# Hybrid decoder layer on one core: the gate projection as one product per k tile, the modulation sums in two halves

## The chip, the cores and the metric

One core of a Trainium2 chip runs the whole layer in one launch. The metric is the device time in microseconds (us) of that launch; three runs were made of the kernel before. Beside them stands one profiled execution with a trace of every instruction.

## What is computed

The layer takes x (256 tokens by 2048), a conditioning vector c and the weights, all float32. Cut to what matters here:

```python
mod = silu(c) @ w_mod + b_mod                  # six sections of 2048
sh_m, sc_m, g_m, sh_f, sc_f, g_f = split(mod, 6)
h = rmsnorm(x, mix_pre_w) * (1 + sc_m) + sh_m
proj = h @ w_in                                # 2048 x 6160
cb, cc, cx, q, k, v, r, a_lr = split(proj)     # a_lr: the last 16 columns
log_a = log_sigmoid(a_lr @ gate_w2 + gate_b) / 16
y = concat(conv(cb, cc, cx), gated_linear_attention(q, k, v, log_a, r)) @ w_out
x = x + g_m * rmsnorm(y, mix_post_w)
x = x + g_f * rmsnorm(conv_ffn(rmsnorm(x) * (1 + sc_f) + sh_f), ffn_post_w)
```

The change touches the 16 columns a_lr (the gate projection) and the place of the sums that turn w_mod's partial products into sh_m and sc_m.

## The kernel before

**Numbers.** Products of large matrices are made from float32 operands split into a high part (rounded to the reduced format float32r by a copy on ScalarE, ACT) and a low part (operand minus high part, a subtraction on VectorE, DVE). A product is then three matmuls on TensorE (PE): high times high, high times low, low times high (L476 to L478 in the input projection). Weights: `high` (L140, ACT, tile `wh`) and `low` (L145, DVE, tile `wl`). Activations: `act_high` (L362, ACT) and `act_low` (L366, DVE) fill the tile `hts[k // 2]`, which holds for each k tile the 256 high columns and, right behind, the 256 low ones.

**Units.** The work is a list of units; `drive` (L69) writes out all instructions in program order, and each engine takes its own in that order. A unit loads a block of weights on SyncE's (SP's) queue two units ahead (`prep`, with the ACT copy), splits it one unit ahead (`low`, DVE), and multiplies (`mm`, PE). Around these stand lists to which other work is hung: `early` (before the next units' prep and low), `pre` (before mm), `mid` (behind mm), then `fin` of the unit before (its results leave PSUM: L402 on DVE), then `late`. So DVE's stream runs one unit ahead of PE's in `low`, and what stands in `late` of unit i stands on DVE behind `low` of unit i + 1.

**Input projection.** The 16 k tiles (128 rows each) are taken in four chunks of 2, 4, 5 and 5 (`CHUNKS`). This text numbers the units: chunk 0 is units 0 to 11, chunk 1 units 12 to 23 (48 matmuls each), chunk 2 units 24 to 41 (45 or 30 matmuls each; unit 24 has 45), chunk 3 units 42 to 59; then 16 units of the output projection (60 to 75), the feed-forward up projection and the down projection. All 12 groups of 512 projection columns stay in SBUF as sums that each chunk adds to.

**Modulation.** While a chunk is multiplied, DVE builds the next chunk's sh_m and sc_m: `mod_steps` multiplies each loaded block of w_mod by a column of silu(c) and adds (L136, into the tile `macc`). Two units before the chunk ends (`LEAD` = 2: units 10, 22 and 40) the 128 partitions are summed by matmuls with a matrix of ones as the moving operand, two columns wide (`products`, L284; `macc` stands as the weights). Each such float32 matmul appears in the trace as two records. `products` for both sections stand in `early` of that unit, ahead of its mm; `columns` (L287, L288, DVE) takes the sums out of PSUM in `late`, and `first` of `modulate_chunk` follows there: PE transposes the normalised x (L347), ACT scales and shifts it (L353) and makes the high part (L362).

**Gate projection.** `second` of `modulate_chunk` multiplies the float32 weights `alr_w` (16 columns) with the float32 activations, one matmul per k tile (L422, two records each), and issues `act_low` (L366) of the chunk. It stands in `late` of the chunk's last unit ahead (units 11, 23, 41); for chunk 0 it stands before the units. `third` (L430, L432, DVE) adds the 16 rows to the tile `alr` in `mid` of the chunk's first unit (12, 24, 42). After chunk 3 the gate steps `gla_gate0` to `gla_gate4` use `alr` with `gate_w2` and a row of ones for `gate_b`.

Of the kernel before, what the change touches and what calls it, by code (L numbers as in the profile page):

```python
# [6 lines left out]
F32 = mybir.dt.float32  # L7
F32R = mybir.dt.float32r
# [6 lines left out]
P = 128  # L15
# [88 lines left out]
def layer_kernel(ctx: ExitStack, tc, x, c, w_mod, b_mod, mix_pre_w, mix_post_w, w_in, conv_w, gate_w2, gate_b,  # L104
# [18 lines left out]
    def slot(shape, dt=F32):  # L123
        return big.tile(shape, dt, tag="big", name=nm("big"))
# [77 lines left out]
    NSV = 58  # L202
    sv_r = const.tile([NSV, P], F32, tag="sv_r", name="sv_r")
    sv = col(NSV, "sv")
# [21 lines left out]
    gla = {}  # L226
    alr_w = const.tile([P, KT, 16], F32, tag="alr_w", name="alr_w")

# [6 lines left out]
    def load_gate():  # L235
        gw = gla["w"] = slot([17, 512])
        nc.gpsimd.dma_start(gw[0:16, :], gate_w2[0])
        nc.gpsimd.dma_start(gw[16:17, :], gate_b)

# [145 lines left out]
    proj = {}  # L385
    alr = const.tile([17, T], F32, tag="alr", name="alr")
    nc.gpsimd.memset(alr, 1.0)
# [16 lines left out]
    def modulate_chunk(ci, ash, early=None):  # L404

        k0, k1 = bounds[ci], bounds[ci + 1]
        kept = []

        def first():
            for kts in pairs(k0, k1):  # L410
                ps = early.pop(0) if early else turn_norm(xs, kts)
                hf = hf0[:, kts[0]:kts[-1] + 1, :] if ci == 0 else hf_tile()
                modulate(ps, kts, ash, CHUNKS[ci], k0, hf)
                for i, k in enumerate(kts):
                    h32.setdefault(ci, {})[k] = hf[:, i, :]
                kept.append((kts, hf, act_high(kts, hf, hts)))

        def second():
            ps = bank([P, T])
            for kts, hf, parts in kept:  # L420
                for i, k in enumerate(kts):
                    nc.tensor.matmul(ps[:16, :], alr_w[:, k, :], hf[:, i, :], start=(k == k0), stop=(k == k1 - 1))  # L422
                if parts:
                    act_low(*parts)
            kept.append(ps)

        def third():
            ps = kept.pop()
            if ci == 0:
                nc.vector.tensor_copy(alr[:16, :], ps[:16, :])  # L430
            else:
                nc.vector.tensor_add(alr[:16, :], alr[:16, :], ps[:16, :])  # L432

        return first, second, third

# [530 lines left out]
    for j, f in enumerate(steps0):  # L966
# [5 lines left out]
        if j in NLD:  # L972
# [5 lines left out]
            nc.scalar.activation(xs[t][1], xs[t][1], AF.Copy, scale=r)  # L978
    nc.sync.dma_start(alr_w, w_in[:, 6144:6160].rearrange("(k p) n -> p k n", p=P))
    small_columns()  # L980
# [5 lines left out]
    columns()  # L986
    for f in modulate_chunk(0, ash, early):
        f()
# [10 lines left out]
    for ci in range(1, len(CHUNKS)):  # L999
# [6 lines left out]
        def cols(ci=ci, n=n, st=st):  # L1006
            st["ash"], products, st["columns"] = mod_columns(st["accs"], n, pre_c[:, bounds[ci]:bounds[ci + 1]], f"ash{ci}")
            products()

        def mod0(ci=ci, st=st):  # L1010
# [265 lines left out]
```

## Time and profile before

| what | us |
|---|---|
| median of 3 runs | 1220.81 |
| lowest, highest | 1220.12, 1221.87 |
| the profiled execution's own time | 1220.69 |
| its span in the trace | 1218.9 |
| PE busy | 1178.1 |
| DVE busy | 947.4 |
| ACT busy | 569.6 |

Times in the trace count from the span's start; 1.8 us of the profiled execution's time lie around the span. Engines: PE is TensorE's matmuls, PEld its weight loads, DVE VectorE, ACT ScalarE, POOL GpSimd, SP SyncE. A row of the timeline gives start, duration, engine, line, operation, output and inputs, shape, count, and in brackets the idle time before it with what ended it. A row of the chain gives start, length, engine and line of merged pieces. A row of the table of windows gives, for a stretch of the span, its length, the busy time and count of PE, PEld, DVE, ACT and POOL, the granted clock of TensorE as a share of full speed, the share of the DMA engines and GB/s. Matmuls are pipelined, so their durations overlap: the pace is the distance between starts.

### The profile page before, as it was taken

The numbers are of one execution on the slowest core, as the hardware profiler recorded it, in microseconds if no ns is written. First come the engines' busy times: TensorE is split into PE (matmuls) and PEld (weight loads), VectorE is DVE, ScalarE is ACT, GpSimd is POOL, SyncE is SP. The second block draws the span as 40 slices with busy tenths as digits, with TensorE's granted clock in tenths as the row PEclk, the third lists the DMA queues.
The fourth block names the chain that finished last, engine by engine and source line by source line (L and its number), as shares of the span: only waits on it lengthen the run. The fifth ranks groups of instructions, "written<-read, shape, count | busy, mean of one in ns | idle before, by whom it ended". The sixth has DMA issues, their size and how long they took to land.

```text
span 1218.9 us, 17103 instructions
## 1 busy us (share of the span) xinstructions
PE 1178.1 (97%) x6993; PEld 1043.1 (86%) x6993; DVE 947.4 (78%) x966; ACT 569.6 (47%) x665; POOL 31.9 (3%) x49
## 2 busy tenths in 40 slices
PE   2999999999999999999999999999999999999997
PEld 1999999999997888888888888888888888888885
DVE  5999899999999877885598979698876664444464
ACT  5553432453474446444564545544545543443442
POOL 2000020000001000000000000000000000000000
PEclk9999999999999998999999999999999999999999
DMA  9999899996699985996766767767674665555522
GB/s 306 385 390 389 306 361 394 397 333 210 203 338 365 341 315 199 355 344 230 240 216 240 249 228 236 261 214 269 220 232 154 241 252 184 204 185 195 199 77 69
DMA packets 128046, 320.73 MB, mean 263 GB/s; under 512 B 8341, under 2 KB 35685, under 8 KB 118240
## 3 DMA queue, kind: packets, MB, share of 16 engines
q1 hardware_dynamic: 125360, 312.63, 72.2%
q0 software_dynamic: 2320, 6.94, 1.5%
q8 instruction: 55, 0.90, 0.3%
q14 instruction: 23, 0.19, 0.0%
q10 hardware_dynamic: 288, 0.07, 0.0%
HBM read 315.42 MB, written 4.19 MB: 262 GB/s over the span
## 4 chain that ended last, share of the span: by engine, by line
PE 94%; DMA 3%; DVE 2%; issue 1%; ACT 0%; SPq 0%; DVEq 0%; ACTq 0%
PE ps L882 27%; PE ps L884 14%; PE ps L741 9%; PE ps L740 9%; PE ps L739 9%; PE ps L476 7%; PE ps L478 7%; PE ps L477 7%; DMA raw<-in_w_mod_dram 2%; PE ps L571 1%; PE ps L473 1%; DVE big L136 1%; PE ps L284 1%; PE ps L422 1%; PE ps L1135 1%
## 5 line engine op out<-in xcount | busy, mean ns | idle before, releaser
L140 ACT CAST wh<-raw 128x2048 fp32r<-128x2048 f32 (+3 forms) x202 | 366.3, 1815 | 507.1 <-PE ps L882 195.3
L145 DVE TENSOR_TENSOR wl<-raw,wh 128x2048 fp32r<-128x2048 f32 (+3 forms) x202 | 437.5, 2167 | 142.3 <-ACT wh L140 142.3
L882 PE MATMUL ps<-big,wh 128*128 128x512 f32 x1400 | 494.8, 398 | 1.8 <-DVE big L366 1.8
L884 PE MATMUL ps<-big,wl 128*128 128x256 f32 x1400 | 393.4, 281 | 0.0
L882 PEld LDWEIGHTS ps<-big,wh 128*128 128x128 f32 x1400 | 263.6, 188 | 65.7 <-DVE big L366 2.1
L884 PEld LDWEIGHTS ps<-big,wl 128*128 128x128 f32 x1400 | 265.2, 189 | 0.0
L478 PE MATMUL ps<-big,wl 128*128 128x256 f32 x733 | 210.0, 286 | 3.5 <-DVE wl L145 3.5
L476 PE MATMUL ps<-big,wh 128*128 128x256 f32 x733 | 211.5, 289 | 0.2 <-ACT wh L140 0.2
L477 PE MATMUL ps<-big,wh 128*128 128x256 f32 x733 | 209.5, 286 | 0.0
L136 DVE SCALAR_TENSOR_TENSOR macc<-raw,c_act,macc 128x2048 f32<-128x2048 f32 (+1 forms) x96 | 199.4, 2077 | 1.8 <-DMA raw<-in_w_mod_dram 1.7
L739 PE MATMUL ps<-wh,big 128*128 128x512 f32 x456 | 178.3, 391 | 0.0
L740 PE MATMUL ps<-wl,big 128*128 128x512 f32 x456 | 177.5, 389 | 0.0
L741 PE MATMUL ps<-wh,big 128*128 128x512 f32 x456 | 177.5, 389 | 0.0
L478 PEld LDWEIGHTS ps<-big,wl 128*128 128x128 f32 x733 | 142.7, 195 | 4.4 <-DVE wl L145 4.4
L476 PEld LDWEIGHTS ps<-big,wh 128*128 128x128 f32 x733 | 142.9, 195 | 2.7 <-ACT wh L140 1.4
L477 PEld LDWEIGHTS ps<-big,wh 128*128 128x128 f32 x733 | 142.9, 195 | 0.1
L740 PEld LDWEIGHTS ps<-wl,big 128*128 128x128 f32 x456 | 85.6, 188 | 18.0 <-issue 0.2
L739 PEld LDWEIGHTS ps<-wh,big 128*128 128x128 f32 x456 | 85.6, 188 | 17.9 <-issue 0.2
L741 PEld LDWEIGHTS ps<-wh,big 128*128 128x128 f32 x456 | 85.6, 188 | 17.7
L136 DVE SCALAR_TENSOR_TENSOR big<-big,fcw,big 128x254 f32<-128x254 f32 (+1 forms) x176 | 72.1, 476 | 0.0
L807 DVE TENSOR_TENSOR big<-big,ps 128x256 f32<-128x256 f32 x88 | 31.1, 416 | 49.1 <-ACT big L805 49.1
L402 DVE TENSOR_TENSOR big<-big,ps 128x512 f32<-128x512 f32 x66 | 43.2, 678 | 1.5 <-PE ps L478 1.5
(183 smaller groups left out, 666.1 us busy)
## 6 DMA issues: line engine op xcount, KB each, us to landing
raw<-in_w_up_dram SPq DMA_DIRECT2D x88, 1024.0 KB, 5.2
raw<-in_w_mod_dram SPq DMA_DIRECT2D x64, 1024.0 KB, 6.6
raw<-in_w_down_dram SPq DMA_DIRECT2D x44, 1024.0 KB, 4.8
raw<-in_w_in_dram SPq DMA_DIRECT2D x24, 960.0 KB, 8.1
raw<-in_w_mod_dram SPq DMA_DIRECT2D x32, 640.0 KB, 7.4
raw<-in_w_out_dram SPq DMA_DIRECT2D x16, 1024.0 KB, 6.6
raw<-in_w_in_dram SPq DMA_DIRECT2D x12, 1024.0 KB, 8.4
raw<-in_w_mod_dram SPq DMA_DIRECT2D x22, 512.0 KB, 6.9
```

The lines of the kernel that those rows point to most:

```text
L136: nc.vector.scalar_tensor_tensor(o, a, s, b, op0=op0, op1=op1)
L140: nc.scalar.copy(hi, raw)
L145: nc.vector.tensor_sub(lo, raw, hi.bitcast(F32))
L402: nc.vector.tensor_add(dst, dst, ps)
L476: nc.tensor.matmul(ps, w[0][:, kk, cs], ht[:, k % 2, 0, :], start=st, stop=False)
L477: nc.tensor.matmul(ps, w[0][:, kk, cs], ht[:, k % 2, 1, :], start=False, stop=False)
L478: nc.tensor.matmul(ps, w[1][:, kk, cs], ht[:, k % 2, 0, :], start=False, stop=sp)
L739: nc.tensor.matmul(ps, a[:, i, 0, ts_], w[0][:, kk, ns], start=st, stop=False)
L740: nc.tensor.matmul(ps, a[:, i, 0, ts_], w[1][:, kk, ns], start=False, stop=False)
L741: nc.tensor.matmul(ps, a[:, i, 1, ts_], w[0][:, kk, ns], start=False, stop=sp)
L882: nc.tensor.matmul(pss[o], wh[:, kk, cs], h2[k // 2][:, k % 2, :, :], start=(first and kk == 0), stop=False)
L884: nc.tensor.matmul(pss[o][:, 1, :], wl[:, kk, cs], h2[k // 2][:, k % 2, 0, :], start=False, stop=(last and kk == 3))
```

## The change

**Gate projection.** The 16 weight columns are split once: `alr_s` holds for each k tile 16 high columns (ACT copy) and 16 low ones (DVE subtraction), made in `early` of unit 1. `second` becomes one float32r matmul per k tile, 32 weight columns against 512 moving columns (256 high and 256 low activations): 16 matmuls in all. The result has 32 rows and two halves; `third` adds both halves to a 32-row `alr` in two DVE operations (one before). `gate_w2` is loaded twice, so that the gate matmul (33 rows instead of 17) adds the four partial products. `act_low` becomes a step of its own (`lows`), where `second` stood.

**Places.** `second` moves from `late` of the unit before the chunk to `mid` of the chunk's first unit (12, 24, 42; for chunk 0: unit 1), since it now needs the low parts; `third` moves from `mid` to `late` of the same unit. The gate steps move on by half a unit to one unit. `products` is called by section: sh_m's sums stay in `early`, ahead of mm of units 10, 22 and 40; sc_m's follow in `mid`, behind mm. Two tiles (`sv_r`, the raw 16 columns) move from a fixed place to the pool of large buffers.

```diff
-    alr_w = const.tile([P, KT, 16], F32, tag="alr_w", name="alr_w")
+    alr_s = const.tile([P, KT, 32], F32R, tag="alr_s", name="alr_s")
+    def split_alr():
+        w = gla["raw"]
+        nc.scalar.copy(alr_s[:, :, 0:16], w)
+        nc.vector.tensor_sub(alr_s[:, :, 16:32], w, alr_s[:, :, 0:16].bitcast(F32))
...
-        def second():
-            ps = bank([P, T])
+        def lows():
             for kts, hf, parts in kept:
-                for i, k in enumerate(kts):
-                    nc.tensor.matmul(ps[:16, :], alr_w[:, k, :], hf[:, i, :], start=(k == k0), stop=(k == k1 - 1))
                 if parts:
                     act_low(*parts)
+        def second():
+            ps = bank([P, 2, T])
+            for k in range(k0, k1):
+                nc.tensor.matmul(ps[:32, :, :], alr_s[:, k, :], hts[k // 2][:, k % 2, :, :],
+                                 start=(k == k0), stop=(k == k1 - 1))
             kept.append(ps)
         def third():
             ps = kept.pop()
             if ci == 0:
-                nc.vector.tensor_copy(alr[:16, :], ps[:16, :])
+                nc.vector.tensor_copy(alr[:32, :], ps[:32, 0, :])
             else:
-                nc.vector.tensor_add(alr[:16, :], alr[:16, :], ps[:16, :])
-        return first, second, third
+                nc.vector.tensor_add(alr[:32, :], alr[:32, :], ps[:32, 0, :])
+            nc.vector.tensor_add(alr[:32, :], alr[:32, :], ps[:32, 1, :])
+        return first, lows, second, third
...
+    chunks[0][1].early.append(split_alr)
+    chunks[0][1].mid.append(second)
+    chunks[0][1].late.append(third)
...
-            products()
+            st["products"]((0,))
...
         us[-LEAD].early.append(cols)
+        us[-LEAD].mid.append(lambda st=st: st["products"]((1,)))
         us[-LEAD].late.append(mod0)
         seconds.append((us[-LEAD + 1].late,
                         lambda st=st: st["m"][1]()))
         seconds.append((chunks[ci][0].mid, lambda st=st: st["m"][2]()))
+        seconds.append((chunks[ci][0].late, lambda st=st: st["m"][3]()))
...
-    tail[0].late.append(gla_gate0)
-    tail[1].late.append(gla_gate1)
-    tail[2].early.append(gla_gate2)
-    tail[2].late.append(gla_gate3)
+    tail[1].mid.append(gla_gate0)
+    tail[2].early.append(gla_gate1)
+    tail[2].late.append(gla_gate2)
+    tail[3].early.append(gla_gate3)
```

**PE at the end of unit 22.** A row is line, operation, output and inputs by tile names, shape and count. `ps_1406` takes unit 22's last products; `ps_1366` takes the modulation sums (`ones` with `macc`); rows with `ident` are the transposes. Before:

```order
L476 MATMUL ps_1406<-big_683,wh_1237 128x256
L477 MATMUL ps_1406<-big_683,wh_1237 128x256
L478 MATMUL ps_1406<-big_683,wl_1303 128x256
L347 MATMUL ps_1438<-ident,big_109 128x128
L347 MATMUL ps_1438<-ident,big_149 128x128
L347 MATMUL ps_1438<-ident,big_109 128x128
```

and now:

```order
L492 MATMUL ps_1406<-big_687,wh_1242 128x256
L493 MATMUL ps_1406<-big_687,wh_1242 128x256
L494 MATMUL ps_1406<-big_687,wl_1308 128x256
L296 MATMUL ps_1366<-ones,macc_619 128x2 x5
L359 MATMUL ps_1443<-ident,big_109 128x128
L359 MATMUL ps_1443<-ident,big_149 128x128
L359 MATMUL ps_1443<-ident,big_109 128x128
```

Five of the ten sum matmuls, which all stood ahead of unit 22, now stand between its last product and the ten transposes; unit 40 reads alike.

**PE around unit 24.** `ps_1526` (before) and `ps_1593` (now) take the gate projection of chunk 2; `ps_1496` is a bank of unit 23, `ps_1544` and `ps_1574` are banks of unit 24. Before, at the end of unit 23:

```order
L477 MATMUL ps_1496<-big_683,wh_1301 128x256
L478 MATMUL ps_1496<-big_683,wl_1379 128x256
L422 MATMUL ps_1526<-hf_1443,alr_w 16x256 x2
L422 MATMUL ps_1526<-hf_1453,alr_w 16x256 x2
L422 MATMUL ps_1526<-hf_1461,alr_w 16x256
L476 MATMUL ps_1544<-big_1446,wh_1377 128x256
```

and now, at the end of unit 24:

```order
L493 MATMUL ps_1574<-big_1468,wh_1377 128x256
L494 MATMUL ps_1574<-big_1468,wl_1474 128x256
L438 MATMUL ps_1593<-big_1451,alr_s 32x512 x2
L438 MATMUL ps_1593<-big_1461,alr_s 32x512 x2
L438 MATMUL ps_1593<-big_1468,alr_s 32x512
L492 MATMUL ps_1574<-big_1451,wh_1472 128x256
```

The gate projection has moved behind the 45 matmuls of unit 24.

**DVE in unit 24.** `wl` rows are the weight splits of units 25 and 26; L402 (now L414) takes unit 23's results out of PSUM; `macc` is a modulation step. Before:

```order
L145 TENSOR_TENSOR wl_1542<-raw_1465,wh_1467 128x1920
L136 SCALAR_TENSOR_TENSOR macc_1293<-raw_1591,c_act,macc_1293 128x1280
L432 TENSOR_TENSOR alr<-alr,ps_1526 16x256
L402 TENSOR_TENSOR big_793<-big_793,ps_1471 128x512
L402 TENSOR_TENSOR big_793<-big_793,ps_1496 128x512
L136 SCALAR_TENSOR_TENSOR macc_1293<-raw_1600,c_act,macc_1293 128x1280
L145 TENSOR_TENSOR wl_1607<-raw_1538,wh_1540 128x1920
```

and now:

```order
L145 TENSOR_TENSOR wl_1541<-raw_1470,wh_1472 128x1920
L136 SCALAR_TENSOR_TENSOR macc_1298<-raw_1590,c_act,macc_1298 128x1280
L414 TENSOR_TENSOR big_796<-big_796,ps_1476 128x512
L414 TENSOR_TENSOR big_796<-big_796,ps_1501 128x512
L447 TENSOR_TENSOR alr<-alr,ps_1593 32x256
L448 TENSOR_TENSOR alr<-alr,ps_1593 32x256
L136 SCALAR_TENSOR_TENSOR macc_1298<-raw_1607,c_act,macc_1298 128x1280
L145 TENSOR_TENSOR wl_1614<-raw_1537,wh_1539 128x1920
```

The addition of the gate projection has become two operations, behind L414 instead of ahead of it; it reads a product that PE makes after unit 24.

More of the change, by code (lines that the diff above doesn't have):

```diff
@@ L202, in layer_kernel @@
     NSV = 58
-    sv_r = const.tile([NSV, P], F32, tag="sv_r", name="sv_r")
+    sv_r = slot([NSV, P])
     sv = col(NSV, "sv")
@@ L226, in layer_kernel, with load_alr @@
     gla = {}
-    alr_w = const.tile([P, KT, 16], F32, tag="alr_w", name="alr_w")
+    alr_s = const.tile([P, KT, 32], F32R, tag="alr_s", name="alr_s")
+    def load_alr():
+        w = gla["raw"] = slot([P, KT, 16])
+        nc.sync.dma_start(w, w_in[:, 6144:6160].rearrange("(k p) n -> p k n", p=P))
+    def split_alr():
+        w = gla["raw"]
+        nc.scalar.copy(alr_s[:, :, 0:16], w)
+        nc.vector.tensor_sub(alr_s[:, :, 16:32], w, alr_s[:, :, 0:16].bitcast(F32))
     def load_small():
@@ L235, in load_gate @@
     def load_gate():
-        gw = gla["w"] = slot([17, 512])
+        gw = gla["w"] = slot([33, 512])
         nc.gpsimd.dma_start(gw[0:16, :], gate_w2[0])
-        nc.gpsimd.dma_start(gw[16:17, :], gate_b)
+        nc.gpsimd.dma_start(gw[16:32, :], gate_w2[0])
+        nc.gpsimd.dma_start(gw[32:33, :], gate_b)
     def load_x(t):
@@ L385, in layer_kernel @@
     proj = {}
-    alr = const.tile([17, T], F32, tag="alr", name="alr")
+    alr = const.tile([33, T], F32, tag="alr", name="alr")
     nc.gpsimd.memset(alr, 1.0)
@@ L986, in layer_kernel @@
     columns()
-    for f in modulate_chunk(0, ash, early):
-        f()
+    first, lows, second, third = modulate_chunk(0, ash, early)
+    first()
+    lows()
     chunks = [in_units(ci) for ci in range(len(CHUNKS))]
+    chunks[0][1].early.append(split_alr)
+    chunks[0][1].mid.append(second)
+    chunks[0][1].late.append(third)
     outs = [out_units(nh) for nh in range(2)]
@@ L1006, in cols @@
         def cols(ci=ci, n=n, st=st):
-            st["ash"], products, st["columns"] = mod_columns(st["accs"], n, pre_c[:, bounds[ci]:bounds[ci + 1]], f"ash{ci}")
-            products()
+            st["ash"], st["products"], st["columns"] = mod_columns(st["accs"], n, pre_c[:, bounds[ci]:bounds[ci + 1]], f"ash{ci}")
+            st["products"]((0,))
         def mod0(ci=ci, st=st):
```

2 lines of the change are left out of this document (1 added, 1 removed).

## The prediction

> **What bounds the kernel now.** I read the chain of work first, then a table of windows over the stages, then DVE's and PE's timelines side by side. The chain names PE, and the windows (length, busy PE, PEld, DVE, ACT, POOL, clock, DMA) name a second full engine:
>
> ```profile
> PE 94%; DMA 3%; DVE 2%; issue 1%; ACT 0%; SPq 0%; DVEq 0%; ACTq 0%
> 75.00:142.00 67.00, 67.00 (x547) 66.81 (x546) 66.74 (x56) 23.98 (x16) 0.00 (x0) 0.97 1.03 382
> 148.00:230.00 82.00, 82.00 (x676) 80.49 (x675) 80.66 (x59) 26.54 (x17) 7.06 (x4) 1.00 1.00 367
> 230.00:295.00 65.00, 64.76 (x497) 61.85 (x497) 63.14 (x60) 28.75 (x31) 3.23 (x3) 0.97 0.90 325
> 295.00:360.00 65.00, 64.76 (x487) 62.56 (x486) 62.65 (x77) 39.28 (x76) 1.10 (x2) 1.00 0.68 237
> 360.00:450.00 90.00, 90.00 (x398) 73.04 (x397) 75.52 (x57) 39.00 (x38) 3.21 (x3) 1.00 0.95 354
> ```
>
> In the stage that the change edits, PE is full, but DVE idles only 0.3 of 67, 1.3 of 82, 1.9 of 65 and 2.4 of 65 us. So the question is how far ahead of PE its weight splits are. Each pair below is a split (L145, or its start and length) and the first matmul that reads it, of units 12, 39, 40 and 60:
>
> ```profile
> 72.43 2.29 DVE L145 TENSOR_TENSOR wl<-raw,wh 128x2048 fp32r<-128x2048 f32 x1
> 75.60 0.28 PE L478 MATMUL ps<-big,wl 128*128 128x256 f32 x1
> 221.36 2.15 DVE L145 TENSOR_TENSOR wl<-raw,wh 128x1920 fp32r<-128x1920 f32 x1
> 223.94 0.28 PE L478 MATMUL ps<-big,wl 128*128 128x256 f32 x1
> 228.56 2.15 DVE L145 TENSOR_TENSOR wl<-raw,wh 128x1920 fp32r<-128x1920 f32 x1
> 231.58 0.28 PE L478 MATMUL ps<-big,wl 128*128 128x256 f32 x1
> 357.75 2.29 DVE L145 TENSOR_TENSOR wl<-raw,wh 128x2048 fp32r<-128x2048 f32 x1
> 360.11 0.49 PE L740 MATMUL ps<-wl,big 128*128 128x512 f32 x1
> ```
>
> The splits are ready at 74.72, 223.51, 230.71 and 360.04, that is 0.88, 0.43, 0.87 and 0.07 us before use. At 360 the two engines meet, and behind it DVE has room (14.5 of 90 us idle). So the end moves by as much as DVE's split of unit 60 moves, whatever PE saves earlier. I follow DVE's lateness, D, to that row.
>
> **What PE saves.** From the chain (start, length, records), gate products (L422), sums (L284) and transposes (L347), and the pace of 512-column and 256-column products:
>
> ```profile
> 73.43 1.83 PE ps L422 x8
> 149.42 2.26 PE ps L422 x10
> 243.05 2.26 PE ps L422 x10
> 133.10 2.13 PE ps L284 x20
> 229.27 2.13 PE ps L284 x20
> 142.57 1.09 PE ps L347 x10
> 360.67 0.40 PE L739 MATMUL ps<-wh,big 128*128 128x512 f32 x1
> 360.91 0.40 PE L740 MATMUL ps<-wl,big 128*128 128x512 f32 x1
> 224.06 0.28 PE L476 MATMUL ps<-big,wh 128*128 128x256 f32 x1
> ```
>
> A product of 512 columns starts 0.24 us after the last, so the new gate products cost 4 x 0.24 = 0.96 and twice 5 x 0.24 = 1.2: PE saves 0.87 + 1.06 + 1.06 = 3.0 us (chunk 0's lie where PE waits for DMA anyway). A 256-column product takes 0.12 (223.94 to 224.06).
>
> The sums cost PE more than their length:
>
> ```profile
> 133.04:136.45 3.41, 3.41 (x32) 3.41 (x31) 3.41 (x3) 1.77 (x1) 0.00 (x0) 1.00 1.02 390
> 136.45:139.87 3.42, 3.42 (x18) 3.42 (x17) 3.42 (x6) 0.00 (x0) 0.00 (x0) 0.50 1.01 363
> 228.62:232.03 3.41, 3.41 (x32) 3.41 (x31) 3.41 (x4) 0.28 (x1) 0.00 (x0) 1.00 1.05 406
> 232.03:235.44 3.41, 3.41 (x18) 3.41 (x17) 3.41 (x3) 1.51 (x1) 0.00 (x0) 0.50 1.04 385
> ```
>
> A stretch of 3.41 us that holds about 2 us of two-column matmuls is followed by one of 3.4 us at a granted clock of 0.50, which loses 1.7 us, twice. Cut in halves (1.07 each, with 5.4 us or more of products between), neither should bring the clock down: another 3.4 us for PE, 6.4 in all, which would end at 1214.3 if PE alone set the time.
>
> **What DVE pays.** Here is DVE, and the one ACT row that matters, where unit 22 gives way to the sums and the high and low parts of chunk 2:
>
> ```profile
> 137.43 0.16 DVE L287 COPY ash<-ps 128x5 f32<-128x5 f32 x1
> 142.61 0.69 DVE L402 TENSOR_TENSOR big<-big,ps 128x512 f32<-128x512 f32 x1 [0.82 <-PE ps L478]
> 143.05 1.02 ACT L353 ACTIVATE hf<-ps,ash 128x256 f32<-128x256 f32 x2 [8.24 <-PE ps L347]
> 144.75 0.69 DVE L366 TENSOR_TENSOR big<-hf,big 128x512 fp32r<-128x512 f32 x1 [1.45 <-ACT big L362]
> 146.33 0.69 DVE L366 TENSOR_TENSOR big<-hf,big 128x512 fp32r<-128x512 f32 x1 [0.88 <-ACT big L362]
> 147.23 0.42 DVE L366 TENSOR_TENSOR big<-hf,big 128x256 fp32r<-128x256 f32 x1 [0.21 <-ACT big L362]
> 147.57 1.54 DVE L136 SCALAR_TENSOR_TENSOR macc<-raw,c_act,macc 128x1280 f32<-128x1280 f32 x1
> 152.56 0.40 DVE L432 TENSOR_TENSOR alr<-alr,ps 16x256 f32<-16x256 f32 x1
> 152.90 1.26 DVE L402 TENSOR_TENSOR big<-big,ps 128x512 f32<-128x512 f32 x2
> ```
>
> Step 1, chunks 0 and 1: the split, and one more addition each. An addition takes 0.34 from start to start (152.56 to 152.90). These hide ahead of step 2, where DVE waits for PE. PE itself reaches unit 13 as before: its 0.87 is eaten, since unit 12's split is ready only 0.88 before use and the gate product now follows unit 12. I take 0; at worst DVE's additions in chunk 0 delay loads by 1 us.
>
> Step 2, unit 22: `columns` waits in DVE's queue for the second half of the sums, behind mm. Behind it are queued the splits of units 24 and 25, and ACT's modulation, which needs `ash`. PE ends unit 22 at 142.57 - 1.07 - 1.7 = 139.8, the half ends at 140.9, `columns` runs at about 141.0 instead of 137.43. The 3.6 us wait replaces the idle time ahead of L402 and L366 (0.82 + 1.45 + 0.88 + 0.21 = 3.36), which goes because ACT's 4.2 us (143.05 to 147.23) now run while DVE does the split. The step at 147.57 stays: D = +0.2, taken as 0.
>
> Step 3, unit 24: the addition now waits for a product behind mm. PE: 140.9, transposes 1.09, unit 23 5.76, unit 24 5.4, gate product 1.2: 154.35. DVE, with L402 ahead, is there at 152.56 + 1.2 = 153.76: a wait of 0.7 with the signal, and 0.34 for the second addition. D = +1.1.
>
> The rest hangs on four idle times or waits that follow:
>
> ```profile
> 173.50 0.69 DVE L402 TENSOR_TENSOR big<-big,ps 128x512 f32<-128x512 f32 x1 [0.64 <-PE ps L478]
> 235.49 0.15 DVE L287 COPY ash<-ps 128x5 f32<-128x5 f32 x1
> 242.85 0.69 DVE L366 TENSOR_TENSOR big<-hf,big 128x512 fp32r<-128x512 f32 x1 [0.69 <-ACT big L362]
> 295.38 1.29 DVE L633 TENSOR_TENSOR big<-big,big 128x512 f32<-128x512 f32 x2 [1.53 <-ACT big L616]
> ```
>
> Step 4: the 0.64 at 173.5 is for PE, now early: D = +0.5. PE's lead of some 2.7 us is spent at units 30 to 40, where DVE gives the pace (0.43 and 0.87 to spare). Unit 40's low products start at 230.71 + 0.5 = 231.2.
>
> Step 5: unit 40 needs 5.2 us from there and its half sum 1.07: `columns` runs at 237.6 instead of 235.49. D = +2.1, less the 0.69 at 242.85: +1.4. Unit 42's product is made at 237.5 + 1.1 (transposes) + 3.6 (30 products) + 5.4 + 1.2 = 248.8; DVE, with L366, a modulation step, a split of 2.15 and L402 still to do from about 244.3, comes to its addition a little later (an estimate from those rows) and does not wait: 0.34 more, +1.75.
>
> Step 6: the 1.53 at 295.38 follows an ACT step queued behind copies for PE's transposes. With PE early and DVE late some 0.9 is left, the way from DVE over ACT and back: D = +1.1 to 1.2 at 360. The gate steps, moved by half a unit, add no instruction; I count them at nothing, as DVE's mask of other work there lasts about as long as ACT's exponential and logarithm.
>
> Sum: 1220.69 + 1.2 = 1221.9, the profiled execution lying 0.1 under the median.
>
> **Rivals.** (a) *Half clock returns, slower.* The second half sum and the transposes now form one stretch of 1.07 + 1.09 = 2.16 us, as long as the old sums. If transposes count as little as the two-column matmuls, the clock halves under units 23 and 41. The first costs step 3 another 1.7 (D +2.8); step 4's 0.64 leaves +2.2; step 5 goes to +3.1 and with the later gate product to +4.2; step 6 leaves +3.3: 1224.0; with one of the two 1223.0 to 1223.5. It decides when over about 1.9 us of that stretch lie in one 3.4 us window. The Trainium skill, page "TensorE: Matmul & The Clock Gate", section "Part 4: PE-mode transpose", says just this: transposes do not count as PE-busy as matmuls do. By that rule the time is rival (a)'s. No row of this trace tests it, since before no transposes adjoin the sums. Chance 0.27.
>
> (b) *PE's saving gets through, faster.* If DVE's waits vanish with PE's lead, D is the two visible additions (0.68) less 0.64, 0.69 and 1.53: -2.2, hence 1218.5; and if units 39 and 60 did not hold PE, 1214.3. Against it: those 0.43 and 0.07 us, and DVE's operations, which last the same throughout (the splits at 221 and 228 both 2.15). Chance 0.12.
>
> (c) *Nothing to be seen.* Steps 3 and 5 cost half of what I take: 1220.9. It is on the same side of the bound as my forecast. Chance 0.13; the forecast itself has 0.48.
>
> **How the numbers follow.** A difference under 0.2% (2.4 us) can't be told from none. The forecast and (c) lie within it, as does a part of (a): same 0.56. (a) above 1223.2, with chunk 0's delay of 1 us on top of the forecast: slower 0.33. From (b), what passes 1218.4: faster 0.11. The range runs from (b)'s first value less the 0.7 by which the lowest run lies under the median, 1217.8, to (a) with that 1 us, 1225.0; the forecast's own is 1220.5 to 1223.3.
>
> **What would show it.** In the profile after: gate products at 0.24 each; no half clock at units 22 and 40 (and (a) if at 23 and 41); DVE waiting for PE at `columns` (about 3.5 and 1.5 us) and at unit 24's addition (0.7); PE waiting for L145 at units 30 to 40, 1 us and more in sum; unit 60's split at about 361.2 and still used at once. The prediction is wrong if that split ends before 358 or its user waits for nothing.

## The result, and the profile after

The change makes the kernel slower: a median of 1226.77 us in 6 runs (1223.75 to 1228.89) against 1220.46 in 6 runs of the kernel before (1216.96 to 1222.39), a ratio of 1.0057 with a 95% interval of 1.0041 to 1.0073. I had forecast +1.2 us; it is +6.3. The profiled execution took 1227.65 us (span 1225.9), 6.96 more than that of before.

The chain of work, its shares by engine, and the same stretches of the table of windows as in the prediction (length, busy PE, PEld, DVE, ACT, POOL, clock, DMA, GB/s):

```profile
PE 79%; DVE 11%; DMA 5%; issue 3%; ACT 1%; SPq 0%; DVEq 0%; ACTq 0%
```

```profile
75.00:142.00 67.00, 66.28 (x537) 65.86 (x538) 63.22 (x53) 24.33 (x16) 0.00 (x0) 0.97 1.01 364
148.00:230.00 82.00, 77.64 (x633) 76.00 (x633) 77.91 (x62) 26.48 (x17) 3.73 (x4) 1.00 0.99 359
230.00:295.00 65.00, 63.25 (x499) 60.88 (x498) 62.04 (x57) 28.63 (x29) 3.22 (x3) 1.00 0.91 327
295.00:360.00 65.00, 64.40 (x481) 61.80 (x480) 62.47 (x75) 33.63 (x70) 1.10 (x2) 1.00 0.69 226
```

PE now idles 4.4 us between 148 and 230, where it idled not at all; DVE idles 3.8 us between 75 and 142 (0.3 before) and 4.1 between 148 and 230 (1.3). Less work on PE, and both engines wait more. The split of unit 60 and its first users, on DVE's and PE's timelines:

```profile
365.62 2.29 DVE L145 TENSOR_TENSOR wl<-raw,wh 128x2048 fp32r<-128x2048 f32 x1
...
365.89 0.48 PE L755 MATMUL ps<-wh,big 128*128 128x512 f32 x1
367.96 0.50 PE L756 MATMUL ps<-wl,big 128*128 128x512 f32 x1 [1.59 <-DVE wl L145]
```

The split ends at 367.91, not 361.2: DVE's lateness there, D, is +7.87 instead of +1.2, and PE stands waiting for it (1.59 us). The time moved by 6.96. So the place that sets the end is the one forecast; what is wrong is the sum of D. Where D comes from, first on PE and DVE at unit 12:

```profile
73.50 0.28 PE L492 MATMUL ps<-big,wh 128*128 128x256 f32 x1
75.72 0.39 PE L493 MATMUL ps<-big,wh 128*128 128x256 f32 x1 [1.94 <-DVE big L378]
...
82.95 1.09 PE L438 MATMUL ps<-big,alr_s 128*32 128x512 f32 x4
83.87 0.28 PE L492 MATMUL ps<-big,wh 128*128 128x256 f32 x1
```

```profile
74.98 1.29 DVE L378 TENSOR_TENSOR big<-hf,big 128x512 fp32r<-128x512 f32 x2
...
84.07 0.41 DVE L447 TENSOR_TENSOR alr<-alr,ps 32x256 f32<-32x256 f32 x1 [2.54 <-PE ps L438]
84.52 0.41 DVE L448 TENSOR_TENSOR alr<-alr,ps 32x256 f32<-32x256 f32 x1
```

The same place on PE and DVE in the kernel before:

```profile
73.36 1.90 PE L422 MATMUL ps<-hf,alr_w 128*16 128x256 f32 x8
75.19 0.39 PE L476 MATMUL ps<-big,wh 128*128 128x256 f32 x1
```

```profile
74.63 1.29 DVE L366 TENSOR_TENSOR big<-hf,big 128x512 fp32r<-128x512 f32 x2
...
81.09 0.40 DVE L432 TENSOR_TENSOR alr<-alr,ps 16x256 f32<-16x256 f32 x1
```

PE's second matmul of unit 12 needs the low activations (L378, before L366). Before, the gate product (L422, 1.83 us) stood here and ran while DVE made them, and the addition (L432) waited for nothing; now PE idles 1.94 us. Then the clock goes down; the table of windows, cut at the edges of the clock's own stretches of 3.41 us:

```profile
72.85:76.26 3.41, 1.47 (x12) 1.26 (x11) 3.41 (x5) 3.38 (x5) 0.00 (x0) 1.00 1.04 389
76.27:79.68 3.41, 3.41 (x18) 3.41 (x17) 3.41 (x2) 2.52 (x4) 0.00 (x0) 0.50 1.04 395
```

A stretch with 1.47 us of PE work is followed by one at 0.50 (18 matmuls, where about 28 fit at 0.12 us each). PE reaches unit 13 at 83.87 (the L492 row above) instead of 81.10. DVE's addition stands in its queue behind that PE and waits 2.54 us, and every later split waits with it. The larger of the other waits of DVE and PE in the stage:

```profile
143.78 0.17 DVE L299 COPY ash<-ps 128x5 f32<-128x5 f32 x1 [2.94 <-PE ps L296]
157.22 0.41 DVE L447 TENSOR_TENSOR alr<-alr,ps 32x256 f32<-32x256 f32 x1 [0.76 <-PE ps L438]
188.27 2.35 DVE L136 SCALAR_TENSOR_TENSOR macc<-raw,c_act,macc 128x2048 f32<-128x2048 f32 x1 [0.34 <-DMA raw<-in_w_mod_dram]
194.66 2.35 DVE L136 SCALAR_TENSOR_TENSOR macc<-raw,c_act,macc 128x2048 f32<-128x2048 f32 x1 [1.98 <-DMA raw<-in_w_mod_dram]
243.19 0.17 DVE L299 COPY ash<-ps 128x5 f32<-128x5 f32 x1 [1.66 <-PE ps L296]
256.30 0.41 DVE L447 TENSOR_TENSOR alr<-alr,ps 32x256 f32<-32x256 f32 x1 [0.88 <-PE ps L438]
303.32 1.30 DVE L649 TENSOR_TENSOR big<-big,big 128x512 f32<-128x512 f32 x2 [0.70 <-ACT big L632]
```

```profile
181.80 0.39 PE L494 MATMUL ps<-big,wl 128*128 128x256 f32 x1 [0.99 <-DVE wl L145]
224.60 0.39 PE L494 MATMUL ps<-big,wl 128*128 128x256 f32 x1 [1.00 <-DVE wl L145]
249.33 0.38 PE L493 MATMUL ps<-big,wh 128*128 128x256 f32 x1 [1.33 <-DVE big L378]
```

At 194.66 it is a load that DVE waits for. Loads are issued when DVE has emptied a buffer; SP's queue, what it waited for between 75 and 145 (sum, times, longest), before:

```profile
SPq L176 <- DVE macc L136: 23.6, 15, 2.2
SPq L453 <- DVE wl L145: 22.9, 11, 3.0
```

and after, where the third row is one load that is held up by unit 12's wait on DVE:

```profile
SPq L176 <- DVE macc L136: 24.7, 16, 2.2
SPq L469 <- DVE wl L145: 22.9, 11, 3.0
SPq L469 <- DVE macc L136: 4.4, 1, 4.4
```

The DMA engines are full in this stage too (shares of 1.01 and 0.99, above), so there are three full engines, not the two that the prediction named. I take it from this that a load that starts late also lands late; no run tests the loads alone.

### The profile page after: what moved, and what is told of

The parts are those of the page before. It is cut to its first block, busy times and chain, and to the rows that moved or that the text cites. A ratio compares the mean times of both kernels' runs of the same rounds, so it can differ in the third digit from the quotient of the medians.

```text
span 1225.9 us, 17083 instructions
## 1 busy us (share of the span) xinstructions
PE 1174.0 (96%) x6977; PEld 1039.0 (85%) x6977; DVE 949.1 (77%) x971; ACT 570.4 (47%) x666; POOL 29.1 (2%) x50
## 4 chain that ended last, share of the span: by engine, by line
PE 79%; DVE 11%; DMA 5%; issue 3%; ACT 1%; SPq 0%; DVEq 0%; ACTq 0%
PE ps L898 27%; PE ps L900 14%; PE ps L757 9%; PE ps L756 9%; PE ps L755 9%; DMA raw<-in_w_mod_dram 5%; DVE macc L136 4%; PE ps L494 3%; PE ps L493 3%; PE ps L492 3%; DVE wl L145 3%; DVE big L136 1%; DVE big L414 1%; PE ps L296 1%; DMA ident<-in_ident_dram 1%
## 5 line engine op out<-in xcount | busy, mean ns | idle before, releaser
L145 DVE TENSOR_TENSOR wl<-raw,wh 128x2048 fp32r<-128x2048 f32 (+3 forms) x202 | 437.6, 2168 | 142.6 <-ACT wh L140 142.6
L492 PE MATMUL ps<-big,wh 128*128 128x256 f32 x733 | 210.5, 287 | 3.0 <-ACT wh L140 3.0
L492 PEld LDWEIGHTS ps<-big,wh 128*128 128x128 f32 x733 | 142.3, 194 | 4.0 <-ACT wh L140 3.1
L843 ACT ACTIVATE big<-big,fcw 128x256 f32<-128x256 f32 x88 | 37.9, 515 | 11.7 <-DVE big L834 11.7
```

The costliest lines, as they stand in the source:

```text
L145: nc.vector.tensor_sub(lo, raw, hi.bitcast(F32))
L492: nc.tensor.matmul(ps, w[0][:, kk, cs], ht[:, k % 2, 0, :], start=st, stop=False)
L843: nc.scalar.activation(st["c"][:, o, :], st["u"][o], AF.Copy, scale=fcw[:, 2, ch + o:ch + o + 1])
```

## The experiments

The theory: DVE sets the end through unit 60's split, and it is late because it stands in its own queue behind PE (at the additions and at the columns), above all because PE idled 1.94 us and lost a half clock at unit 12, where the old gate product had covered the low activations. The rivals: DVE's added instructions and the loads (1); PE's work as such (2). Each kernel's lateness D, in us against the kernel before, is read from the ends of the splits (L145) in its profiled execution. The forecast is the prediction's; a dash is a row that it has no value for. The last two rows are the profiled time less 1220.69 (in the first column that of the forecast) and the ratio to the kernel before over all runs (half widths of the intervals 0.0011 to 0.0019). There is one trace of each kernel.

| D at unit | forecast | after | e1 | e2 | e3 | e4 | e5 | e6 | e7 | e8 | e9 | e12 |
|---|---|---|---|---|---|---|---|---|---|---|---|---|
| 12 | - | 0.34 | 0.01 | 0.15 | 0.62 | 2.43 | 0.66 | 0.15 | 0.25 | 1.71 | 0.05 | 0.79 |
| 14 | 0 | 3.42 | -0.09 | 1.72 | 0.63 | 4.01 | 1.13 | 0.05 | 0.33 | 1.63 | 0.06 | 1.20 |
| 25 | 0 | 2.63 | 0.79 | 0.92 | 0.50 | 1.88 | 0.34 | 2.43 | -0.07 | 1.74 | -1.15 | -0.29 |
| 26 | 1.1 | 3.91 | 0.46 | 4.66 | 0.50 | 4.55 | 1.62 | 2.62 | -0.11 | 1.41 | -1.48 | -0.62 |
| 36 | 0.5 | 5.97 | 1.48 | 5.17 | 2.11 | 5.46 | 2.12 | 3.00 | 0.91 | 1.95 | -0.98 | 0.26 |
| 43 | 1.4 | 6.94 | 2.45 | 6.14 | 3.09 | 4.68 | 3.10 | 3.98 | 1.88 | 1.69 | -1.25 | -0.03 |
| 44 | 1.75 | 8.36 | 2.12 | 8.18 | 3.09 | 6.08 | 3.54 | 5.39 | 2.32 | 1.37 | 0.46 | -0.35 |
| 48 | - | 8.81 | 4.31 | 8.62 | 3.09 | 6.53 | 3.61 | 5.84 | 2.37 | 1.37 | 0.90 | 0.73 |
| 60 | 1.2 | 7.87 | 3.39 | 7.66 | 2.16 | 5.60 | 2.69 | 4.92 | 1.45 | 0.47 | -0.03 | -0.22 |
| time | 1.2 | 6.96 | 3.43 | 6.85 | 3.21 | 5.32 | 1.75 | 6.86 | 0.88 | -0.53 | -0.29 | -0.21 |
| ratio | 1.0010 | 1.0057 | 1.0048 | 1.0066 | 1.0011 | 1.0054 | 1.0029 | 1.0044 | 1.0021 | 0.9992 | 1.0007 | 0.9994 |

The row at unit 12 is what an execution brings along from chunk 0. In e4 (2.43) and e8 (1.71) that is much, in part by longer waits of DVE for loads between 60 and 72 (2.64 and 1.96 us in sum, 1.37 in the kernel before). So D at unit 14 is to be read against that row, and a difference of some 2 us between two single traces need not come from an edit.

The row at unit 60 and the row of the time belong together: in ten of the eleven kernels the time follows D within 1.1 us, and in e6 within 2.0. The rest goes with the clock behind 450 us, in a part that none of the edits touches: stretches of 3.41 us at 0.50 between 450 and 490 number 3 before, and 1 to 3 in the others (time less D: with 1 stretch -0.8 to -1.0, with 2 -0.6 to 0.0, with 3 -0.3 to 1.9).

### e1: the additions half a unit later

```diff
-        seconds.append((chunks[ci][0].late, lambda st=st: st["m"][3]()))
+        seconds.append((chunks[ci][1].pre, lambda st=st: st["m"][3]()))
```

> The changed kernel with the additions of the gate product (DVE) moved half a unit on, behind the next weight split (units 13, 25, 43 instead of 12, 24, 42). Theory: what makes DVE late is that it stands in its queue behind PE: at the additions of unit 12 (2.54 us), at the columns of unit 22 (2.94), at the additions of units 24 and 42 (0.76, 0.88). With the additions later their waits shrink to under 0.4 each, and the split of unit 14 ends at about 85.7 instead of 88.6; but PE is as late as before at unit 22 (lost 1.94 us and a half clock at unit 12), so the wait for the columns grows by as much and DVE's lateness at unit 25 stays about 2.6; behind it 1.0 less at unit 26, about 1.5 less in waits for loads at 175 to 200, 1.1 less at unit 42: lateness at unit 60 about 4.3 instead of 7.9, time 1223.3. Rival 1 (DVE's added instructions and the loads, not the waits): nothing changes by more than 0.5, 1226.5. Rival 2 (PE's own lost time at unit 12 sets the end): 1226.5 as well, with the lateness at unit 60 as it was.

Measured: 1225.94 us, ratio 1.0048 (1.0029 to 1.0067). I had expected 1223.3; the median is nearer to the 1226.5 of the two rivals, and it can't be told from the changed kernel, so the time of e1 decides nothing. Its trace shows the waits: those at the additions are gone and D at unit 14 is -0.09. At unit 25 it is 0.79, less than I expected. From unit 44 to 48 it grows by 2.19: 0.77 for the additions, which now stand behind the split of unit 44, and 1.42 with the gate's later steps, which now wait 1.33 us for ACT. PE idles 1.80 us at unit 12 as it did, but no half clock follows, and PE reaches unit 13 only 0.94 later than before (2.77 in the changed kernel). The table of windows, at the clock's edges of this execution:

```profile
71.11:74.52 3.41, 2.47 (x21) 2.27 (x19) 3.41 (x2) 3.35 (x7) 0.00 (x0) 1.00 1.04 389
74.53:77.94 3.41, 2.56 (x21) 2.56 (x22) 3.41 (x5) 2.61 (x3) 0.00 (x0) 1.00 1.05 392
```

The edge falls into the wait, and each side keeps 2.5 us of work. So a wait of 1.9 us costs PE another 1.7 or nothing, by where it falls. The profiled execution took 1224.12, near the lowest of this kernel's five times (1223.63 to 1228.49), so the D of this one trace lies below what the median stands for.

### e2: the cover put back

```diff
+            if ci:
+                ps = bank([P, T])
+                for kts, hf, parts in kept:
+                    for i, k in enumerate(kts):
+                        nc.tensor.matmul(ps[:16, :], alr_s[:, k, 0:16].bitcast(F32), hf[:, i, :],
+                                         start=(k == k0), stop=(k == k1 - 1))
```

> The changed kernel with a product added that nobody reads: 16 weight columns in float32 by the float32 activations, where the gate product stood before the change (ahead of units 12, 24 and 42). It only covers the time in which DVE makes the low parts of the activations. Theory: PE's wait of 1.94 us for the low parts at unit 12 and the half clock behind it (76.3 to 79.7) are gone although PE has 6 us more work; PE reaches unit 13 about 1 us later than in the kernel before, not 2.8; the addition of unit 12 waits about 0.7 instead of 2.54; lateness of DVE at unit 14 about 1.6 instead of 3.4, at unit 25 about 1 instead of 2.6, at unit 60 about 5 instead of 7.9; time about 1224.5. Rival 1 (DVE's added instructions and the loads): no change at unit 60, 1226.5. Rival 2 (PE's total work sets the end): 6 us more work makes it slower, 1229 or more.

Measured: 1227.60 us, ratio 1.0066 (1.0047 to 1.0085). At unit 12 all is as the theory has it: PE does not wait there, no half clock, the addition waits 0.99 instead of 2.54, D is 1.72 at unit 14 and 0.92 at unit 25. The end is a miss (7.66 instead of 5): the 2.26 us of covering work ahead of unit 24, where nothing needed cover, delay the gate product there. DVE's timeline:

```profile
82.37 0.41 DVE L453 TENSOR_TENSOR alr<-alr,ps 32x256 f32<-32x256 f32 x1 [0.99 <-PE ps L444]
157.97 0.41 DVE L453 TENSOR_TENSOR alr<-alr,ps 32x256 f32<-32x256 f32 x1 [3.21 <-PE ps L444]
```

The addition of unit 24 waits 3.21 instead of 0.76, and D is 4.66 at unit 26. What is won at one wait behind PE is lost here at the next.

### e3 and e4: each half of the change alone

e3 is the kernel before with the split of the sums:

```diff
-            products()
+            st["products"]((0,))
...
         us[-LEAD].early.append(cols)
+        us[-LEAD].mid.append(lambda st=st: st["products"]((1,)))
```

> The kernel before with only the second half of the modulation sums moved behind the unit's products (units 10, 22, 40). Theory: the columns wait 3.6 us for PE at unit 22 and about 1.5 at unit 40, which takes the place of DVE's idle time for the low parts (3.4 and 0.7); lateness at unit 25 about 0.2, at unit 60 about 1; no half clock at units 22 and 40, and the 3.4 us that PE saves there do not reach the end: time 1221.5. Rival 1: the same within 0.5. Rival 2 (PE sets the end): 1217.

e4 is the changed kernel with that taken back (whole sums in `early`):

> The changed kernel with the modulation sums whole again ahead of units 10, 22 and 40; the gate product stays as changed. Theory: the half clock is back at units 22 and 40, the columns do not wait; DVE is as late as in the changed kernel at unit 14 (3.4, from the addition behind the gate product) and at unit 26 (about 4, since the low parts now wait for a late PE); about 1 us less at unit 42; lateness at unit 60 about 7, time 1226. So most of the slowdown belongs to the gate product's place, little to the sums. Rival 1: the same. Rival 2 (PE sets the end): 3.4 us slower than the changed kernel, 1230. Rival 3 (the split of the sums is the cause): back to 1221.5.

Measured: e3 1220.98, ratio 1.0011 (0.9999 to 1.0022); e4 1225.88, ratio 1.0054 (1.0036 to 1.0072). In e3 the columns of unit 22 wait 3.52 us and D at unit 25 is 0.50, so step 2 of the prediction holds; PE's 3.4 us of saved half clocks do not reach the end, against rival 2. (The profiled execution of e3 was the slowest of its ten.) e4 is as slow as the changed kernel within what these runs tell apart: by the times, the slowdown belongs to the gate product. The trace of e4 is not what I had expected: it brings 2.43 along from chunk 0, PE idles only 1.04 us at unit 12, and the whole sums bring no half clock at units 22 and 40; D grows by 1.58 up to unit 14 and by 2.67 at unit 26, where the addition waits 2.15 for PE.

### e5: low activations last in the first unit of a chunk

```diff
+                if ci and tiles[0] == 24:
...
+                    for sub in (tiles[::2], tiles[1::2]):
+                        for a, b in ((0, 0), (1, 0), (0, 1)):
+                            for nt in sub:
```

> The changed kernel; in the first unit of chunks 1, 2 and 3 (units 12, 24, 42) the products with the low activations come last within each pair of column tiles, so that PE has work while DVE makes the low parts. The same products, in another order. Theory: PE's wait of 1.94 us at unit 12 falls to 0.6 (it then waits for the low weights) and that at unit 42 (1.33) goes; no half clock at 76; the addition of unit 12 waits about 0.8 instead of 2.54; lateness of DVE at unit 14 about 1.6 (now 3.4), at unit 25 about 0.9 (2.6), at unit 60 about 4.5 to 5 (7.9): time 1224. Rival 1 (DVE's added instructions and the loads set the lateness): unit 60 within 0.5 of 7.9, 1226.7.

Measured: 1222.46, ratio 1.0029 (1.0015 to 1.0044): half of the slowdown is gone, with the same instructions in another order, more than I expected (1224). On PE's and DVE's timelines a wait of 1.02 us is left (for ACT's high part, where I had 0.6 for the low weights), no half clock follows, and the addition waits for nothing:

```profile
75.05 0.98 PE L489 MATMUL ps<-big,wh 128*128 128x256 f32 x6 [1.02 <-ACT big L374]
...
81.78 0.41 DVE L447 TENSOR_TENSOR alr<-alr,ps 32x256 f32<-32x256 f32 x1
```

D at unit 25 is 0.34 (2.63 in the changed kernel), and from 43 to 44 it grows by 0.44 instead of 1.42, as unit 42's wait (1.33) is gone too. This is the run that shows the lost cover as a cause: rival 1 expected no change.

### e6 and e7: the gate products summed in one bank

```diff
         def second():
-            ps = bank([P, 2, T])
+            if ci == 0:
+                gla["sum"] = bank([P, 2, T])
+            ps = gla["sum"]
             for k in range(k0, k1):
                 nc.tensor.matmul(ps[:32, :, :], alr_s[:, k, :], hts[k // 2][:, k % 2, :, :],
-                                 start=(k == k0), stop=(k == k1 - 1))
+                                 start=(k == 0), stop=(k == KT - 1))
```

with the copy and one addition in unit 42 alone. e7 has this and e5's order.

> The changed kernel with the gate products of all four chunks summed in one PSUM bank that is held from unit 1 to unit 42; the two additions on DVE are done once, in unit 42 (a copy and an addition), and are gone from units 1, 12 and 24. PE works as in the changed kernel. Theory: nothing on DVE waits for PE at units 12 and 24 any more: lateness at unit 14 about -0.3 (now 3.4). What PE loses at unit 12 shows at the columns of unit 22 instead: at unit 25 about 0.8 if no half clock follows that loss, 2.6 if one does; from there no more at unit 26, 1 to 2 more up to unit 36 (waits for loads), 1 at unit 42, 1.4 at unit 44: unit 60 at 3 to 5, time 1223 to 1225. Rival 1 (loads): 1226 or more. If the bank that is held makes PE wait for a free one, PE shows waits for DVE's evacuations that the changed kernel has not.

> The last two together: low activations last in units 12, 24 and 42, and the gate products summed in one bank. Theory: lateness at unit 14 about -0.3, at unit 25 about 0.3, up to 1.5 at unit 36, 2.5 at unit 42 after the columns, at unit 60 about 2: time 1222, between the kernel before and the changed one, since the columns' waits and one copy and addition at unit 42 remain. Rival 1: 1226. Rival 2 (PE sets the end; it has saved 6 us against the kernel before): 1215.

Measured: e6 1224.91, ratio 1.0044 (1.0026 to 1.0062); e7 1221.61, ratio 1.0021 (1.0007 to 1.0035). e6 tells the two parts of unit 12's loss apart. Without the additions D is 0.05 at unit 14, and yet 2.43 at unit 25. Windows of the clock and DVE's timeline of e6:

```profile
72.76:76.17 3.41, 1.57 (x13) 1.37 (x13) 3.41 (x4) 3.38 (x5) 0.00 (x0) 1.00 1.05 396
76.18:79.59 3.41, 3.41 (x18) 3.41 (x18) 3.41 (x2) 2.57 (x4) 0.00 (x0) 0.50 1.04 394
```

```profile
143.58 0.17 DVE L299 COPY ash<-ps 128x5 f32<-128x5 f32 x1 [5.80 <-PE ps L296]
```

PE lost its 1.84 us and the half clock again, and the columns of unit 22 collect it: they wait 5.80 us instead of 2.94. So it is PE's loss at unit 12 that costs, here at the next place where DVE stands behind PE. With the loss taken away as well (e7) D is -0.07 at unit 25. PE shows no wait for a free bank in either.

### e8: no gate product at all

> The kernel before with the gate products (L422) and their additions left out (the gate is then computed from constants): PE has 6.9 us less work and DVE 1.1, and the products no longer cover the low parts at units 12, 24 and 42. It bounds what any cheaper gate product can bring here. Theory: PE waits about 1.9 us for the low activations at unit 12 and 1 to 1.5 at unit 42; lateness of DVE at unit 60 between -1.5 and 0, time 1219 to 1220. Rival 2 (PE sets the end): 1213.

Measured: 1219.34, ratio 0.9992 (0.9978 to 1.0007), no difference that can be told. The edit takes the L422 matmuls and the L430 and L432 additions out. DVE's split of unit 60 and its user:

```profile
358.22 2.28 DVE L145 TENSOR_TENSOR wl<-raw,wh 128x2048 fp32r<-128x2048 f32 x1
360.56 0.50 PE L732 MATMUL ps<-wl,big 128*128 128x512 f32 x1 [1.06 <-DVE wl L145]
```

PE has over 6 us less to do (the L422 rows of chunks 1 to 3 in the prediction, 1.83 + 2.26 + 2.26; the expectation's 6.9 adds chunk 0) and gets none of it to the end; rival 2 (1213) is out. With the other work in this order, a cheaper gate product could bring here no more than these runs tell apart (0.22% at most). D at unit 60 is 0.47, somewhat above what I expected; 1.71 stood at unit 12 already. PE waits 2.16 us for the low activations at unit 12, as the theory has it, and since the clock's edge at 75.85 cuts that wait in two, no half clock follows.

### e9 and e12: a version without the waits

e9 is e7 with the sums whole. e12 also moves what stands on DVE behind the gate in chunk 3:

```diff
-        seconds.append((chunks[ci][0].late, lambda st=st: st["m"][3]()))
+        seconds.append((chunks[ci][1].pre, lambda st=st: st["m"][3]()))
...
-    tail[3].early.append(gla_gate3)
+    tail[3].pre.append(gla_gate3)
```

> The kernel of e7 (low activations last in units 12, 24 and 42; gate products summed in one bank) with the modulation sums whole again ahead of units 10, 22 and 40. Theory: the columns no longer wait behind PE (1.66 us at unit 40 in e7), the half clock is back at units 22 and 40, which PE can bear now; lateness of DVE at unit 25 about 0.3, at unit 60 about 0.5 instead of 1.45: time 0.5 us over the kernel before. Rival 2 (PE sets the end): 3.4 us slower than e7.

> The kernel of e9 with its last two waits behind the gate moved under weight splits: the copy and addition of the gate sums stand behind the split of unit 44 instead of unit 43's, and the gate step that waits for the logarithm (0.36 us) behind the split of the next unit. Theory: the wait of 1.17 us at unit 42 and the 0.36 are gone; DVE's lateness at unit 60 goes from 0.0 in e9 to -1.5, and since PE waits 1.59 us there in e9 (it has work saved) the end follows: 1 to 1.5 us faster than the kernel before. Rival 2 (DVE is not what holds PE at unit 60): as e9, 0.5 us slower than before. Rival 5 (the wait for ACT at 295, 0.70 in e9, grows by what is gained): unit 60 at 0.0, as e9.

Measured: e9 1220.48, ratio 1.0007 (0.9995 to 1.0018); e12 1219.11, ratio 0.9994 (0.9980 to 1.0007). With the waits gone the new gate product costs nothing, as expected of e9, though at unit 25 it does better than I expected (-1.15): the half clock that I had expected at units 22 and 40 came back at unit 40 alone. e12 removes its two waits (no row of DVE between 243 and 295 waits over 0.25 us, where e9 waits 1.17 and 0.36), and from unit 43 to 48 D grows by 0.76 instead of 2.15; but this execution came to unit 43 1.2 later than e9's, with more waits for loads from 63 to 83, so D at unit 60 is -0.22 and not -1.5. The median is 0.5 us under the kernel before, which these runs can't tell from none. None of my versions beats the kernel before.

### e10 and e11: five weight splits on GpSimd

```diff
-        nc.vector.tensor_sub(lo, raw, hi.bitcast(F32))
+        (eng or nc.vector).tensor_sub(lo, raw, hi.bitcast(F32))
```

> The kernel of e9 with five weight splits (units 32, 35, 50, 54 and 58; 2.15 us each on DVE) done on GpSimd, which is idle. Theory: DVE has 10.8 us less to do; its split of unit 60 ends 2 us or more earlier than in the kernel before, its user no longer waits, and what is left of PE's saving reaches the end: 1.5 to 2 us faster than the kernel before. Rival 1 (loads: the stretch from 165 to 240 is bound by them): DVE waits for loads instead, the same as e9. Rival 4: GpSimd takes over 5 us for a split and slows DVE down while it runs; PE waits for it, slower than e9.

> The kernel before with the same five weight splits on GpSimd. Theory: there PE and DVE come to unit 60 together, so DVE's relief alone brings nothing: unit 60's split ends 2 us or more earlier, the first matmul that reads it starts within 0.5 us of 360.1, the time stays within 0.5 us. Rival (DVE alone sets the end there): 2 us faster or more. Rival 4 (GpSimd's splits are too slow or hold DVE up): slower.

Measured: e10 1229.37, ratio 1.0070 (1.0050 to 1.0089); e11 1227.05, ratio 1.0061 (1.0046 to 1.0076). Both are slower, as rival 4 had it. A GpSimd split and the DVE step beside it, and the same step in the kernel before:

```profile
182.73 4.71 POOL L145 TENSOR_TENSOR wl<-raw,wh 128x1920 fp32r<-128x1920 f32 x1 [21.89 <-ACT wh L140]
```

```profile
183.75 5.85 DVE L136 SCALAR_TENSOR_TENSOR macc<-raw,c_act,macc 128x2048 f32<-128x2048 f32 x1
```

```profile
183.83 2.35 DVE L136 SCALAR_TENSOR_TENSOR macc<-raw,c_act,macc 128x2048 f32<-128x2048 f32 x1
```

DVE's step ends 2.2 us after GpSimd's split does, at 189.60, about its own length alone: it seems to have stood still until then. DVE saves 2.15 and loses 3.5. At unit 60 D is 9.43 in e10 and 8.91 in e11. The Trainium skill, page "SBUF — State Buffer", section "Who interferes with whom", says that a DVE instruction with two inputs in SBUF contends with a GpSimd instruction that reads SBUF, and that the ports they share are an exclusive lock; this row agrees. So what a relief of DVE would bring was not measured here.

## Why the prediction was wrong

**What bounds the kernel.** Right: the end moves with unit 60's split (table above), and PE's saving ahead of it is lost (e3, e8). Left out: the DMA engines as the third full one.

**What PE saves.** Right in size: the next matmul starts 0.92 us after the first of four gate products (0.96 forecast), and units 22 and 40 have no half clock. But whole sums do not always bring one (none in e4, one in e9), so the 3.4 us is what one execution had to save.

**Step 1, chunks 0 and 1: the step that failed, and whose cause the runs show.** It reads "PE itself reaches unit 13 as before ... I take 0". PE reached it 2.77 late and D became 3.4 at unit 14 and 2.63 at unit 25. The step priced the gate product where it went and not the place that it left: it had covered the low activations. For PE the step added up -1.83 (the old product gone), +0.87 (the wait for the weight split) and +0.96 (the new product behind unit 12), which is 0. The trace has -1.83 + 1.94 + 0.96 + 1.70 = 2.77: the wait ends with the low activations and is 1.07 longer, and the half clock, the larger part, was not in the sum at all. (In e1, which has the wait and not the half clock, the same sum gives 0.93, and PE was 0.94 late.) The half clock comes or not by where the wait falls in time, so this part of the loss differs between executions. And the step let the additions "hide" in a queue that stands behind PE. Shown by e5 (cover: 0.34 at unit 25), e6 (PE's loss apart from the additions: 2.43) and, at unit 12 itself, e2.

**Step 2, columns of unit 22.** Right as a step: a wait of 2.94 (3.5 forecast) takes the place of the idle time; e3 has 3.52 and D +0.50.

**Step 3, unit 24.** Right: a wait of 0.76 (0.7), D +1.28 (+1.1).

**Step 4: the other step that failed, by as much.** PE did lose its lead at units 30 to 40 (0.99, 1.29, 1.00, 1.08 and 0.42 us for L145, where I had "1 us and more"), but D went up by 2.06 instead of down by 0.6: the 0.64 vanished, and waits for loads of 0.74, 0.34 and 1.98 came. In the other kernels of the table this stretch (unit 26 to 36) costs 0.4 to 1.6, so the -0.6 came true in none. The cost does not follow how late DVE comes to it: e2 comes 4.66 late and pays 0.51, e3 comes 0.50 late and pays 1.61. So late issue of the loads does not explain it by itself, and the cause stays open; no run held the loads alone.

**Step 5, units 40 and 42.** The columns: D +0.97, as worked out (+0.9). The addition of unit 42 "does not wait": it waited 0.88, since PE had lost 1.33 us for the low activations, the same missing cover. 1.42 instead of 0.34.

**Gate steps, counted at nothing.** They cost 0.45 at unit 46, a wait of 0.36 for ACT's logarithm and its signal.

**Step 6.** -0.94 (forecast -0.6): 0.70 of the 1.53 is left.

In sum 2.63 + 1.28 + 2.06 + 0.97 + 1.42 + 0.45 - 0.94 = 7.87. Of the 6.7 that the forecast lacks, steps 1 and 4 hold 2.6 each and unit 42 holds 1.1.

**Rivals.** (a) did not happen: no half clock under units 23 and 41. (b) and (c) were wrong as well. The outcome lies above the range, because its upper end was built from the waits that I had listed, and neither the lost cover nor the loads of step 4 were among them. The signs named for being wrong (the split of unit 60 before 358, or a user that waits for nothing) looked only for an end that comes early; it came late.

## What to carry to other kernels

When an instruction is moved, price the place that it leaves as well: see what its engine comes to next there, and which other engine's result that needs at once. Where two engines are both full, expect a wait of one in its queue for the other to be paid where the two meet, unless an idle time on the way takes it up, and work saved on one alone to be worth little (over 6 us of PE work taken away moved this kernel by less than its runs can tell). Let an instruction that reads another engine's result stand some work behind it in its queue, and order the products so that the operand that is ready last is used last.

## What the runs showed of the hardware

**A half clock after a wait of 1.9 us.** Stretches of 3.41 us lie on a grid of their own in each execution. One with 1.47 or 1.57 us of PE work is followed by one at 0.50; those of e1 with 2.47 and 2.56, and of e8 with 2.26 and 2.19, are not:

```profile
72.44:75.85 3.41, 2.26 (x17) 1.86 (x15) 3.41 (x5) 2.98 (x6) 0.00 (x0) 1.00 1.04 390
75.86:79.27 3.41, 2.19 (x18) 2.19 (x19) 3.41 (x5) 2.98 (x4) 0.00 (x0) 1.00 1.05 392
```

The Trainium skill, page "TensorE: Matmul & The Clock Gate", section "What's actually happening", has windows of 3413 ns that run freely, as here; it lets the clock fall after a whole idle window, and here one less than half full was enough.

**Whole sums bring the clock down only at some places in time.** Seven kernels have the sums whole (before, e4, e8 to e12), at units 22 and 40 each. In 8 of these 14 places a half clock follows: there a stretch holds 1.26 to 1.36 us of other products, the rest sums. In the 6 others the stretch keeps 1.49 to 2.06 us of products. With the sums in halves (the seven other kernels) it never follows at these units. The shares are worked out from the starts of PE's rows in each trace.

**Transposes keep the clock up.** Rival (a) rested on transposes counting as little as two-column sums. In the changed kernel one stretch holds 1.03 us of sums (142.57 to 143.60), then transposes to its end, and 1.45 us of other products, no more than the stretch that brought the clock down at unit 12. The table of windows for it and the next:

```profile
141.12:144.53 3.41, 3.41 (x33) 3.41 (x32) 0.75 (x3) 0.25 (x1) 0.00 (x0) 1.00 0.99 363
144.54:147.95 3.41, 3.41 (x31) 3.41 (x30) 3.41 (x3) 3.35 (x7) 1.48 (x3) 1.00 0.45 102
```

The clock stays at 1.00. A closer pair: in e5 the stretch from 139.23 to 142.64 holds 1.33 us of products, 1.03 of sums and 1.05 of transposes, and the next is at 1.00; in the kernel before, the one from 133.04 to 136.45 holds 1.36 of products and 2.05 of sums, and the next is at 0.50. So these transposes count, at least in part; the rule quoted with rival (a) does not hold for them.
